# A two-layer hybrid mixer trunk on one core: operations recorded first, then issued in the order of a list scheduler inside the kernel

## Chip, cores and metric

One core of one Trainium2 chip. The metric is the device time of one execution in microseconds, as the median of three runs. All inputs and outputs are float32.

## What is computed

Two layers. Each normalises x (512 tokens, 1024 channels), projects it with one matrix, runs four mixers on their own columns, gates each with a SiLU path, projects the concatenation back and adds it to x. A last normalisation ends it.

```python
def hybrid_layer(x, norm_w, w_in, w_out, conv_w, pe_cmp, w_cmp_k, w_cmp_v, pool_w, pool_scale):
    h = rmsnorm(x, norm_w)
    p = split_cols(h @ w_in)
    o_a = dsa_mixer(...)        # ReLU indexer, 8 heads -> top 128 keys of each query -> softmax attention, 4 heads
    o_b = nsa_mixer(...)        # compressed blocks + selected blocks + window of 512, sigmoid gates, 4 heads
    o_c = shortconv_mixer(...)  # b * conv3(c * x)
    o_d = pool_mixer(...)       # causal means over 2, 4, 8, 16 tokens, minus the token, a linear map per group
    mixed = concatenate([silu(gate) * o for each of the four])
    return x + mixed @ w_out

def reference(x, ...):
    for l in range(2):
        x = hybrid_layer(x, ...)
    return rmsnorm(x, final_norm_w)
```

## The kernel before

The engines are PE (matmuls and transposes), DVE (VectorE), ACT (ScalarE), POOL (GpSimd) and SP, which issues all DMAs. Tokens lie in four tiles of 128. A float32 product of good accuracy is made of three matmuls: every operand is split into a high part (a rounded copy, type float32r) and a low part (the difference, made by `lo`), and high x high, high x low and low x high are added up in PSUM (`lin_tok`, L129, and `lin_ch`, L141).

`load_w` (L98) brings a group of weight columns in four parts: SP loads into a staging tile `st` (four places), ACT copies the high part `wh`, POOL subtracts the low part `wl` (six places each). A staging place is free again when POOL has subtracted.

A layer runs in this program order. `projections` (L678) goes through four groups of columns and, within each, through the four token tiles, four at a time in flight: `group_a` (queries and key of mixer A, index key), `group_idx` (index queries, then per head one score matmul, a relu on ACT into a tile `rl`, two places, and a multiply-add on DVE into `acc`), `group_bk` and `group_bq` (keys, values and queries of mixer B). Then come `compress`, `gates`, and the attention calls `att_a(i)` and `att_b(i)` of token tile i, mixed with `topk` (16 rounds of max and match-replace on DVE over `acc`), `conv` and `conv_gate_pool`. `probs` (L501) makes a call's probabilities in tiles `pb` of the tag `big` (ten places): score matmuls on PE, a reduction on DVE (L519), an exponential on ACT (L521), a reciprocal chain on DVE (L522 to L525), a scaling on POOL (L528). `pv` (L531) transposes them on PE, splits them on ACT and DVE, and multiplies by the values; `finish` (L543) gates the result into `mT`. `att_a(i)` for i > 0 needs `topk(i)`.

At the end of a layer the residual tiles `x` (eight of `big`) and the next norm's gain `g` (two of `rl`) are loaded, and `w_out` is applied in three chunks of columns. In layer 0 the sum goes to `x1d` in DRAM, and each token tile is normalised for layer 1 (`norm_tile`). In layer 1 it is normalised and stored.

The program order is only a wish: the tile framework, which was started with `schedule_with_timeline_sim=True` (L793), orders each engine's instructions by its own model of their durations, and gives a tile one of its tag's places when it comes to it. Nothing moves at run time: each engine runs its list in order, with semaphore waits.

## Time and profile before

| what | value |
|---|---|
| median of three runs | 569.18 us (567.56 to 570.59) |
| the profiled execution, its own time | 571.24 us |
| its span, first to last instruction | 569.5 us |
| mean granted TensorE clock | 0.98 |
| DMA | 51.14 MB, mean 90 GB/s |

The profile counts an engine as busy while one of its instructions runs. Matmuls overlap each other, so a busy PE is not a PE at its peak rate. "Granted clock" is the share of TensorE's full clock that was let through. Behind an instruction group stands the idle time of the engine just before it, and who ended it. The slices of the page (40 equal ones, in tenths) show the shape of the run:

```profile
PE   6989799989999999989999988999999999989995
DVE  3856889999998988963175869999999999795533
PEclk8899989998999999999999989999999999999999
```

### The profile page before, as it was taken

What the parts mean: (1) busy time and instruction counts of PE and PEld (TensorE: products, weight loads), DVE (VectorE), ACT (ScalarE), POOL (GpSimd) and SP (SyncE); (2) the same over time, 40 slices, a digit from 0 to 9 for tenths busy, and PEclk for the clock granted to TensorE, in tenths of its full rate; (3) what the DMA queues carried; (4) which work ended last, traced back from release to release, by engine and by line L of the source; (5) the groups of instructions that cost most, each with busy time, mean ns of one, the idle gap of its engine ahead of it and who ended that gap; (6) DMA issues with size and microseconds to landing.
All of it is one profiled execution on the core that took longest, in us unless ns stands there. A gap on an engine that the chain in (4) does not pass through costs nothing.

```text
span 569.5 us, 9672 instructions
## 1 busy us (share of the span) xinstructions
PE 533.6 (94%) x3076; PEld 469.3 (82%) x3076; DVE 449.4 (79%) x1152; ACT 319.8 (56%) x797; POOL 298.9 (52%) x398
## 2 busy tenths in 40 slices
PE   6989799989999999989999988999999999989995
PEld 5889798768887878779999978886788888878895
DVE  3856889999998988963175869999999999795533
ACT  3466955363645756673345686636544675766243
POOL 4855633473726384551855637427553649454252
PEclk8899989998999999999999989999999999999999
DMA  8632211382313020425722513117513212042303
GB/s 258 201 94 56 64 30 39 83 203 67 75 38 75 20 92 13 138 76 164 196 77 60 135 52 92 39 22 195 137 38 75 55 58 86 28 129 74 111 2 147
DMA packets 70370, 51.14 MB, mean 90 GB/s; under 512 B 19248, under 2 KB 64432, under 8 KB 70320
## 3 DMA queue, kind: packets, MB, share of 16 engines
q1 hardware_dynamic: 70320, 50.54, 32.1%
q8 instruction: 24, 0.39, 0.3%
q14 instruction: 26, 0.21, 0.1%
HBM read 46.33 MB, written 4.19 MB: 89 GB/s over the span
## 4 chain that ended last, share of the span: by engine, by line
PE 60%; DVE 26%; ACT 5%; DMA 3%; issue 2%; POOL 1%; SPq 1%; POOLq 0%; ACTq 0%; DVEq 0%
PE mm L137 9%; PE mm L139 9%; PE mm L138 8%; PE mm L147 7%; PE mm L149 7%; PE mm L148 7%; DVE acc L346 4%; DVE m L345 4%; DVE acc L335 4%; PE tr L535 3%; PE pv L541 2%; PE pv L540 2%; PE s L516 2%; PE s L515 2%; ACT wh L122 2%
## 5 line engine op out<-in xcount | busy, mean ns | idle before, releaser
L95 POOL TENSOR_TENSOR wl<-st,wh 128x768 fp32r<-128x768 f32 (+4 forms) x94 | 161.1, 1734 | 73.6 <-ACT wh L122 63.8
L147 PE MATMUL mm<-hT,wh 128*128 128x512 f32 x272 | 109.4, 402 | 3.0 <-DVE sg L499 1.5
L149 PE MATMUL mm<-hT,wl 128*128 128x512 f32 x272 | 108.3, 400 | 0.8 <-POOL wl L95 0.8
L148 PE MATMUL mm<-hT,wh 128*128 128x512 f32 x272 | 108.4, 399 | 0.0
L528 POOL TENSOR_SCALAR pb<-pb,rs 128x512 f32<-128x512 f32 (+3 forms) x96 | 52.9, 568 | 88.6 <-DVE rs L525 38.3
L521 ACT ACTIVATE pb<-pb,mn 128x512 f32<-128x512 f32 (+3 forms) x96 | 53.7, 559 | 66.7 <-DVE mn L519 63.8
L137 PE MATMUL mm<-wh,hT 128*128 128x360 f32 (+3 forms) x240 | 76.0, 319 | 7.8 <-ACT hT L252 4.2
L122 ACT ACTIVATE wh<-st 128x768 fp32r<-128x768 f32 (+4 forms) x92 | 70.5, 775 | 15.8 <-PE mm L139 7.7
L139 PE MATMUL mm<-wh,hT 128*128 128x360 f32 (+3 forms) x240 | 75.9, 316 | 1.2 <-DVE hT L95 1.2
L138 PE MATMUL mm<-wl,hT 128*128 128x360 f32 (+3 forms) x240 | 75.1, 314 | 0.0
L147 PEld LDWEIGHTS mm<-hT,wh 128*128 128x128 f32 x272 | 51.8, 190 | 14.2 <-DVE sg L499 1.7
L137 PE MATMUL mm<-wh,mT 128*128 128x384 f32 (+1 forms) x192 | 62.0, 324 | 1.0 <-ACT mT L552 0.5
L139 PE MATMUL mm<-wh,mT 128*128 128x384 f32 (+1 forms) x192 | 61.0, 319 | 0.9 <-DVE mT L95 0.9
L138 PE MATMUL mm<-wl,mT 128*128 128x384 f32 (+1 forms) x192 | 61.6, 321 | 0.0
L149 PEld LDWEIGHTS mm<-hT,wl 128*128 128x128 f32 x272 | 51.7, 190 | 11.7 <-POOL wl L95 1.7
L148 PEld LDWEIGHTS mm<-hT,wh 128*128 128x128 f32 x272 | 51.7, 190 | 9.8 <-issue 0.2
L137 PEld LDWEIGHTS mm<-wh,hT 128*128 128x128 f32 x240 | 47.3, 198 | 9.4 <-ACT hT L252 4.7
L345 DVE MAX8 m<-acc 128x8 f32<-128x384 f32 (+2 forms) x96 | 52.2, 551 | 0.4
L346 DVE MATCH_REPLACE8 acc<-m,acc 128x384 f32<-128x384 f32 (+2 forms) x96 | 51.9, 541 | 0.1
L139 PEld LDWEIGHTS mm<-wh,hT 128*128 128x128 f32 x240 | 47.2, 197 | 2.0 <-DVE hT L95 2.0
L95 DVE TENSOR_TENSOR pl<-tr,ph 128x512 fp32r<-128x512 f32 x60 | 40.6, 683 | 10.2 <-ACT ph L538 10.1
L138 PEld LDWEIGHTS mm<-wl,hT 128*128 128x128 f32 x240 | 47.2, 197 | 0.2
(194 smaller groups left out, 1163.9 us busy)
## 6 DMA issues: line engine op xcount, KB each, us to landing
st<-in_w_in_dram SPq DMA_DIRECT2D x104, 128.0 KB, 2.7
st<-in_w_in_dram SPq DMA_DIRECT2D x28, 256.0 KB, 3.3
st<-in_w_out_dram SPq DMA_DIRECT2D x16, 384.0 KB, 3.4
x<-in_x_dram SPq DMA_DIRECT2D x16, 256.0 KB, 4.0
st<-in_w_in_dram SPq DMA_DIRECT2D x8, 320.0 KB, 4.7
st<-in_w_out_dram SPq DMA_DIRECT2D x8, 256.0 KB, 2.9
x1d<-x SPq DMA_DIRECT2D x8, 256.0 KB, 2.0
x<-x1d SPq DMA_DIRECT2D x8, 256.0 KB, 3.2
```

Source lines behind the costliest of these rows:

```text
L95: eng.tensor_sub(dst, src, f(hi))
L122: S.activation(wh[:, :, :n], st[:, :, :n], AF.Copy)
L137: PE.matmul(ps[:, :n], act[0][:, k, ts], rh, start=st, stop=False)
L138: PE.matmul(ps[:, :n], act[0][:, k, ts], rl, start=False, stop=False)
L139: PE.matmul(ps[:, :n], act[1][:, k, ts], rh, start=False, stop=sp)
L147: PE.matmul(ps, lh, act[0][:, k, :], start=k == 0, stop=False)
L148: PE.matmul(ps, lh, act[1][:, k, :], start=False, stop=False)
L149: PE.matmul(ps, ll, act[0][:, k, :], start=False, stop=k == KC - 1)
L345: V.max(m8, a)
L346: V.match_replace(a, m8, a, MARK)
L521: S.activation(p, p, AF.Exp, scale=-1.0, bias=mn[:, h : h + 1], accum_out=rs[:, h : h + 1])
L528: G.tensor_scalar(p, p, rs[:, h : h + 1], 0.0, op0=OP.mult, op1=OP.add)
```

## The change

The kernel now writes a tape. `Tape.record` takes every call to an engine, notes the tiles and the regions that it reads and writes, and makes it wait for the earlier operations that touch the same regions. `Tape.cost` gives each a duration. `Tape.schedule` then picks, again and again, for each engine the recorded operation that can start soonest; among those that can start within 1 ns of that, the one that stands first in program order. `Tape.play` issues the calls in this order, with the framework's own ordering off (`tc.manual_schedule()`).

A tile no longer has a pool's place that the framework hands out, but a slot of its tag, a tag and pool entry of its own, that the scheduler binds when the first operation on it is picked. `Place.safe` lets a tile take a slot ahead of earlier ones only as long as each tile that stands before it in program order can still get one. Weights are recorded where they are first used (`Weights`), and the loads of the compression weights moved from `compress` to `compressed`. In the changed kernel every instruction carries the line of `play`, L422.

```diff
+class Place:
+    def __init__(self, pool, tag, bufs):
+        self.pool, self.tag, self.bufs = pool, tag, bufs
+        self.free = [0.0] * bufs
+        self.holds = [None] * bufs
+        self.waiting = []
+
+    def safe(self, t):
+
+        for k, y in enumerate(self.waiting):
+            if y is t:
+                return True
+            live = sum(1 for h in self.holds if h is not None and h.last >= y.first)
+            live += sum(1 for z in self.waiting[:k] if z.last >= y.first)
+            if live + 2 > self.bufs:
+                return False
...
+class Weights:
+    def __getitem__(self, h):
+        if h not in self.parts:
+            self.parts[h] = self.part(h)
+        return self.parts[h]
...
+SEM = 52
...
+    def cost(self, op):
...
+                if dt == F32R:
+                    op.occ = max(112, m * 0.4375 + 5)
+                    op.seen = m * 0.4375 + 205
...
+        elif op.eng == "ACT":
+            op.dur = (170 if psum else 295 if op.args[2] == AF.Exp else 205) + 0.835 * n
+            op.occ = op.dur - 100
...
+            elif op.name == "tensor_tensor_reduce":
+                op.dur = 208 + 1.04 * n
+                op.occ = op.dur - 84
+            elif op.name in ("tensor_scalar", "tensor_copy") and not psum:
+                op.dur = 146 + 0.52 * n
+                op.occ = op.dur - 84
+                op.locks = True
+            else:
+                op.dur = (215 if op.name == "scalar_tensor_tensor" and not psum else 150) + 1.04 * n
+                op.occ = op.dur - 84
+                op.locks = two
...
+    def schedule(self):
...
+        def candidate(e):
+            best = None
+            soonest = 1e18
+            found = []
+            for op in ready[e]:
+                s = slots(op)
+                if s is None:
+                    continue
+                s = max(s, op.ready, free[e])
+                found.append((s, op))
+                soonest = min(soonest, s)
+            for s, op in found:
+                if s <= soonest + 1 and (best is None or op.num < best[1].num):
+                    best = (s, op)
+            return best
...
+            s, e = min(have)
+            op = cand[e][1]
+            if op.locks:
+                s = max(s, lock["POOL"])
+            if e == "POOL":
+                s = max(s, lock["DVE"])
+            op.start = s
+            if op.locks:
+                lock["DVE"] = s + op.dur
+            if e == "POOL":
+                lock["POOL"] = s + op.dur
+            free[e] = s + op.occ
...
+    def play(self):
+        for op in self.schedule():
+            def real(v):
+                return v.real() if isinstance(v, View) else v
+
+            getattr(self.engines[op.eng].real, op.name)(*[real(a) for a in op.args],
+                                                        **{k: real(v) for k, v in op.kw.items()})
...
-    nc = tc.nc
+    tape = Tape(tc.nc)
...
+    class Pool:
+        def tile(self, shape, dtype, name, tag=None, bufs=None):
+            return tape.tile(self, shape, dtype, name, tag or name, bufs or self.bufs)
...
-        parts = []
...
-        for h in range(4):
+        def part(h):
...
-            parts.append((wh, wl))
-        return parts
+            return wh, wl
+
+        return Weights(part)
...
-        compressed(*cmp_in)
+        compressed(cmp_in)
...
     for l in range(DEPTH):
         st = layer(l, *st)
+    with tc.manual_schedule():
+        tape.play()
```

## The prediction

> **What bounds the kernel now.** First the page's busy table, then the same by stage (windows: length, busy time and instruction count of PE, PEld, DVE, ACT, POOL, then granted clock, DMA share, GB/s).

> ```profile
> PE 533.6 (94%) x3076; PEld 469.3 (82%) x3076; DVE 449.4 (79%) x1152; ACT 319.8 (56%) x797; POOL 298.9 (52%) x398
> ...
> 0.00:30.00 30.00, 23.52 (x124) 21.86 (x125) 18.92 (x32) 13.32 (x36) 19.42 (x44) 0.89 0.76 227
> 30.00:100.00 70.00, 63.47 (x413) 59.18 (x412) 56.19 (x142) 46.61 (x124) 34.06 (x55) 0.98 0.21 54
> 100.00:250.00 150.00, 143.91 (x764) 117.78 (x763) 136.74 (x370) 85.28 (x202) 81.14 (x90) 0.98 0.30 80
> 250.00:330.00 80.00, 79.22 (x527) 77.18 (x525) 41.91 (x93) 39.97 (x108) 44.13 (x57) 1.00 0.45 127
> 330.00:350.00 20.00, 16.64 (x106) 15.59 (x107) 14.83 (x32) 17.22 (x50) 12.91 (x21) 0.91 0.25 66
> 350.00:500.00 150.00, 147.04 (x788) 122.68 (x788) 142.60 (x398) 86.08 (x201) 81.21 (x93) 1.00 0.28 73
> 500.00:550.00 50.00, 46.51 (x259) 41.97 (x258) 31.75 (x74) 25.11 (x64) 20.10 (x30) 1.00 0.27 82
> 550.00:569.50 19.50, 13.29 (x107) 13.09 (x105) 6.50 (x16) 6.26 (x17) 5.91 (x12) 0.94 0.29 108
> ```

> PE is the bound: idle for only 569.5 - 533.6 = 35.9 us of its span. But the second bound is close. In the two attention stages (100 to 250 in layer 0, 350 to 500 in layer 1) DVE is busy 91% and 95%, so PE and DVE are both nearly full there. In 30 to 100, 330 to 350 and 500 to 550 neither is full: there each waits for the other's answers, which is where an order of issue can lose or win. Of the idle time 6.5 us lie in the first 30 us (waiting for the first loads) and 6.2 us in the last 19.5 (the last tiles' scaling and store). The other 23.2 us are 6.5, 6.1, 0.8, 3.4, 3.0 and 3.5 us, row by row.

> Then one such wait from close by: DVE and PE on the timeline around 70 us (start, length, what, and in brackets the idle time before and who ended it), and the windows over the three stretches of low clock after the start.

> ```profile
> 62.39 0.48 DVE L335 SCALAR_TENSOR_TENSOR acc<-rl,wi,acc 128x256 f32<-128x256 f32 x1
> ...
> 65.44 1.87 DVE L335 SCALAR_TENSOR_TENSOR acc<-rl,wi,acc 128x256 f32<-128x256 f32 x1
> ...
> 67.80 1.48 DVE L335 SCALAR_TENSOR_TENSOR acc<-rl,wi,acc 128x256 f32<-128x256 f32 x1
> 69.31 0.42 DVE L95 TENSOR_TENSOR kTB<-tr,kTB 128x256 fp32r<-128x256 f32 x1
> ...
> 69.79 0.44 PE L415 MATMUL tr<-ident,z 128*128 128x128 f32 x2 [1.54 <-DVE kTB L95]
> ...
> 71.75 0.44 PE L415 MATMUL tr<-ident,z 128*128 128x128 f32 x2 [1.08 <-DVE qiT L95]
> ...
> 72.30:75.80 3.50, 3.50 (x16) 3.50 (x15) 3.50 (x12) 1.04 (x3) 1.69 (x5) 0.51 0.33 75
> 126.90:133.80 6.90, 6.54 (x20) 5.24 (x20) 6.90 (x20) 1.78 (x5) 5.86 (x6) 0.51 0.47 109
> 331.70:335.20 3.50, 3.36 (x15) 3.36 (x16) 2.70 (x8) 3.12 (x11) 1.44 (x5) 0.51 0.02 5
> ```

> The same multiply-add of 128x256 takes 0.48 us once and 1.87 and 1.48 us a moment later, so something outside DVE holds it. Behind it in DVE's queue stands the 0.42 us subtraction that frees a transpose bank, and PE, whose next instruction needs that bank, idles 1.54 us and soon 1.08 us more. Right after it the granted clock is 0.51 for 3.5 us. The three stretches are 13.9 us at half rate, so they cost 13.9 x 0.49 = 6.8 us: 1.7, 3.4 and 1.7. An order that avoids the short waits also saves these.

> [...]

> **The change part by part.** It adds and drops no arithmetic: the same matmuls, DVE, ACT and POOL operations, the same DMAs. Both programs are statically ordered per engine; what changes is the order, and which tile gets which buffer when.

> (1) The order by fitted durations. Place one, PE in layer 0, at the wait of 69.8 us: block key transposes (`tr<-ident,z`), index scores (`s<-kiT,qiT`), projections (`mm`). Before:

> ```order
> L332 MATMUL s_777<-kiT_180,qiT_709 128x384
> L415 MATMUL tr_956<-ident,z_918 128x128 x2
> L332 MATMUL s_782<-kiT_180,qiT_709 128x384
> L332 MATMUL s_787<-kiT_180,qiT_710 128x384
> L415 MATMUL tr_1050<-ident,z_961 128x128 x2
> L137 MATMUL mm_1108<-wh_1025,hT_139 128x320
> ```

> Now:

> ```order
> L422 MATMUL mm_954<-wh_679,hT_192 128x268
> L422 MATMUL tr_992<-ident,z_879 128x128 x2
> L422 MATMUL mm_954<-wh_679,hT_181 128x268
> L422 MATMUL s_1002<-kiT_426,qiT_780 128x384
> L422 MATMUL mm_954<-wl_698,hT_181 128x268
> L422 MATMUL mm_954<-wh_679,hT_192 128x268
> ```

> Before, two pairs of transposes that need DVE's answers stood almost back to back; now 20 projection matmuls and one score stand between this pair and the next. Such waits are what this part can remove. Outside the attention stages the idle time is 6.5 + 0.8 + 3.4 + 3.5 = 14.2 us, and two of the low-clock stretches lie there, 1.7 + 1.7 = 3.4 us: 17.6 us together. I take three quarters, 13 us (10.6 of waits, 2.6 of clock): the waits are of order, but new ones will come. Bounds: nothing, and 17.6 us. In the attention stages there are 6.1 + 3.0 us of idle PE and 3.4 us of clock, 12.5 us. DVE is 91 and 95% full there and does the same work after as before, so I take 2 us, with the bounds nothing and 12.5. What holds DVE (the 1.87 us) stays: the new scheduler reckons with it, but does not choose around it, since it adds that delay after it has chosen.

> (2) Buffers taken early. Place two, SP's queue in layer 0, after the query weights; `x` are the residual tiles that the output projection adds at the end of the layer (before they were issued 43 rows later, behind the output weights), `g` the next norm's gain. Before:

> ```order
> L111 DMA st_1043<-in_w_in_dram 128x2x64
> L447 DMA pet_1300<-in_pe_cmp_dram 16x2x64
> L111 DMA st_1247<-in_w_in_dram 128x2x128
> L111 DMA st_1247<-in_w_in_dram 128x2x256
> L111 DMA st_1254<-in_w_in_dram 128x2x128
> ```

> Now:

> ```order
> L422 DMA pet_455<-in_pe_cmp_dram 16x2x64
> L422 DMA x_463<-in_x_dram 128x512
> L422 DMA x_469<-in_x_dram 128x512
> L422 DMA x_480<-in_x_dram 128x512
> L422 DMA x_493<-in_x_dram 128x512
> L422 DMA x_509<-in_x_dram 128x512
> L422 DMA x_523<-in_x_dram 128x512
> L422 DMA g_535<-in_norm_w_dram 128x512
> L422 DMA pet_782<-in_pe_cmp_dram 16x2x64
> L422 DMA st_877<-in_w_in_dram 128x2x128
> ```

> Six residual tiles and a gain now stand ahead of the compression weights (`st_877`). The transfers are cheap: six of 256 KB while the DMA engines are 21% busy. They hold buffers, though: 6 of the 10 `big` places and 1 of the 2 `rl` places until the layer's end, and in layer 1 the reads of `x1d` do the same. So the four 512-wide probability tiles of one attention call fill all that is left, and relu (ACT) and multiply-add (DVE) of the index scores share one buffer. Prices, from the groups by form (count, busy us, mean ns of one):

> ```profile
> L519 DVE CUSTOM_DVE_ANT_0 pb<-s,acc 128x512 f32<-128x512 f32 x8 | 5.5, 689 | 2.8 <-PE s L516 2.7
> L521 ACT ACTIVATE pb<-pb,mn 128x512 f32<-128x512 f32 x24 | 17.3, 722 | 21.1 <-DVE mn L519 21.1
> L521 ACT ACTIVATION_READ_ACCUMULATOR pb<-pb,mn 128x1 f32 x96 | 18.1, 189 | 0.0
> L522 DVE TENSOR_SCALAR rs<-rs 128x4 f32<-128x4 f32 x24 | 12.6, 523 | 1.6 <-ACT pb L521 1.5
> L523 DVE RECIPROCAL rs<-rs 128x4 f32<-128x4 f32 x24 | 4.1, 170 | 0.2
> L528 POOL TENSOR_SCALAR pb<-pb,rs 128x512 f32<-128x512 f32 x24 | 16.3, 696 | 31.2 <-DVE mx L590 11.6 <-DVE rs L523 10.0 <-DVE rs L525 8.8
> L95 DVE TENSOR_TENSOR pl<-tr,ph 128x512 fp32r<-128x512 f32 x60 | 40.6, 683 | 10.2 <-ACT ph L538 10.1
> L546 ACT ACTIVATE ob<-pv 64x512 f32<-64x512 f32 x16 | 9.5, 595 | 10.5 <-PE pv L541 8.3 <-PE pv L602 1.8
> L334 ACT ACTIVATE rl<-s 128x256 f32<-128x256 f32 x16 | 6.2, 389 | 0.2
> L334 ACT ACTIVATE rl<-s 128x384 f32<-128x384 f32 x16 | 7.9, 492 | 7.4 <-PE s L332 6.0 <-DVE acc L335 1.4
> L334 ACT ACTIVATE rl<-s 128x512 f32<-128x512 f32 x16 | 9.5, 594 | 2.4 <-PE s L332 2.2
> L335 DVE SCALAR_TENSOR_TENSOR acc<-rl,wi,acc 128x256 f32<-128x256 f32 x14 | 11.7, 836 | 0.5 <-ACT rl L334 0.3
> L335 DVE SCALAR_TENSOR_TENSOR acc<-rl,wi,acc 128x384 f32<-128x384 f32 x14 | 10.3, 734 | 1.1 <-ACT rl L334 1.1
> L335 DVE SCALAR_TENSOR_TENSOR acc<-rl,wi,acc 128x512 f32<-128x512 f32 x14 | 11.5, 821 | 0.0
> ```

> With one `rl` buffer the relu no longer runs under the multiply-add: per layer 8 x (0.389 + 0.492 + 0.594) = 11.8 us more in a chain of 8 x (0.836 + 0.734 + 0.821) = 19.1 us. I cost it at nothing: DVE is 56.19 of 70 us busy there, its own other work fills the gaps, and PE has projections left. With that cover gone, it is 11.8 us a layer, and top-k of tile 1 is late next.

> Place three, DVE in layer 0, between the third and the fourth tile's attention on selected keys (`att_a(2)`, `att_a(3)`; `ISA pb,mn<-s,acc` is the reduction of the scores). Before:

> ```order
> L551 SCALAR_TENSOR_TENSOR om_2149<-om_2149,sg_1480 128x256
> L522 TENSOR_SCALAR rs_2463<-rs_2463 128x4
> L523 RECIPROCAL rs_2463<-rs_2463 128x4
> L95 TENSOR_TENSOR mT_1246<-om_2149,mT_1245 128x2x128
> L519 ISA pb_2917,mn_2921<-s_2923,acc_847 128x512
> L519 ISA mn_2921 128x1
> ```

> Now:

> ```order
> L422 TENSOR_TENSOR pl_2963<-tr_2926,ph_2937 128x512
> L422 TENSOR_TENSOR cd_2897<-cd_2917,tab 128x16
> L422 TENSOR_TENSOR om_2983<-pv_2912,ob_2974 64x256 x2
> L422 TENSOR_TENSOR cd_2897<-cd_2897,cd_2880 128x16
> L422 SCALAR_TENSOR_TENSOR om_2983<-om_2983,sg_1399 128x256
> L422 SCALAR_TENSOR_TENSOR cd_2917<-cd_2917,mm_2878 128x512
> L422 ISA pb_2995,mn_2996<-s_2960,acc_1246 128x512
> ```

> Before, tile 3's reductions followed tile 2's reciprocal almost at once; now they come after tile 2's transposes, products and gate. Tile 3's chain, now alone: 4 x 0.69 + 0.72 + 0.19 + 0.52 + 0.17 + 0.70 + 4 x 0.68 + 0.60 = 8.4 us per layer. I cost it at nothing, since PE still has the last convolution gate and half of the output projection's matmuls then, and tile 2's scores stand 47 rows earlier in PE's queue than before. If that cover fails it is 8.4 us a layer, 16.8 in all; the last token tile's output projection is late next.

> At the layer boundary two reads of `x1d` now stand in SP's queue ahead of the last of layer 1's first weights, and each must wait until the store before it has landed:

> ```profile
> x1d<-x SPq DMA_DIRECT2D x8, 256.0 KB, 2.0
> ```

> That is 2 x 2.0 = 4 us for the queue. I cost it at nothing, because PE is busy 79.22 of 80 us there with output projection; were that cover gone, it is 4 us, once, and layer 1's first projection is late next.

> Recording, constants set earlier on POOL and the weights asked for at first use cost nothing: POOL is idle 10.6 of the first 30 us.

> **The sum.** 13 + 2 = 15 us off. The profiled execution took 571.24 us with a span of 569.5, 2.1 us above the median 569.18; taken from the median, the forecast is **554 us**, own range 539 (all 30.1 us of movable idle and clock) to 569 (none).

> **The rivals.**

> First, DVE sets the time: the attention stages stay as they are, and what is won elsewhere only lets DVE's queue start waiting earlier. For it: 91 and 95%. Against it: outside of attention DVE is 56.19 of 70, 14.83 of 20 and 31.75 of 50. Time: only the 2 us, 567.

> Second, held buffers. One place, the end of each layer's attention: tile 3 starts its reductions only when tile 2's four places are free, PE runs out of matmuls that do not need tiles 2 and 3, and DVE has no top-k left. For it: the rows of place three, and 500 to 550, where PE already loses 3.5 us at this place. Against it: PE's cover. It decides from the point where the chain, 8.4 us, outlasts PE's other work. With it the relu chain of one buffer is exposed to a third, 2 x 11.8 / 3 = 7.9. Time: 569.2 + 16.8 + 7.9 - 13 = 581.

> Third, the fit is better than I grant, and all 30.1 us go. For it: the durations in the new cost table are near the rows here (208 + 1.04 x 512 ns = 0.74 us for the 512-wide reduction, beside 0.69 above). Against it: two engines that are both over 90% full seldom leave no gap. Time: 539.

> Fourth, the change doesn't do what it says: a greedy order that fails on the chip where DVE is held from outside: new waits replace old ones one for one. Time: 569.

> **How the numbers follow.** Forecast 0.52, better fit 0.13, DVE or one for one 0.11, held buffers 0.24. Within 0.5% (566.3 to 572.0, about what this measurement can tell from no change) fall DVE's case and the one-for-one case, 0.11 together; faster is 0.52 + 0.13 = 0.65; slower 0.24. The range is 539 to 579: it leaves out the lower half of the better fit and about half of the held buffers.

> **What would show it.** Right: PE idle in 30 to 100 and about 330 to 350 shrinks by some 10 us, at most one half-rate stretch after the start, DVE's attention stages as long as before. Wrong: ACT's relu waiting for DVE's multiply-add in the waits view, DVE's reductions waiting for PE's transposes, or an idle PE just ahead of the last token tile's output projection. A PE span that shrinks by over 25 us would say that attention was not bound by DVE.

## The result, and the profile after

The changed kernel takes 596.11 us (594.85 to 598.99) where the kernel before takes 569.88 in the same session: a ratio of 1.0467, interval 1.0407 to 1.0526. It is 26 us slower, and outside the predicted range. The profiled execution took 594.85 us with a span of 593.1.

The page of the changed kernel: busy time by engine, and the slices of PE, DVE and the granted clock.

```profile
PE 547.8 (92%) x3076; PEld 470.2 (79%) x3076; DVE 428.1 (72%) x1152; ACT 320.8 (54%) x797; POOL 302.5 (51%) x398
...
PE   7997999999999789999999789999999899898995
...
DVE  4764689989899898452374658899998978475423
...
PEclk9996999999999899999999979999999979898999
```

DVE is busy 21.3 us less than before (449.4), for the same operations (e1 below, the new machinery with the old order, has 448.9): the new order avoids some of the holds (83 DVE instructions take over 1.25 times the median of their form before, 65 now; they stand 68.5 and 49.0 us above it in all). Nothing came of it. PE idles 593.1 - 547.8 = 45.3 us instead of 35.9, and what it does it does at a lower clock (mean 0.969, before 0.980). By stage (window, length, busy time and count of PE, PEld, DVE, ACT, POOL, clock, DMA share, GB/s):

```profile
30.00:100.00 70.00, 63.70 (x391) 57.16 (x389) 50.51 (x124) 45.42 (x122) 37.95 (x56) 0.93 0.30 81
100.00:250.00 150.00, 140.03 (x709) 109.30 (x709) 130.72 (x370) 80.70 (x189) 75.92 (x84) 0.99 0.26 67
250.00:330.00 80.00, 77.53 (x504) 74.49 (x504) 39.38 (x91) 39.15 (x105) 42.48 (x58) 1.00 0.44 129
330.00:350.00 20.00, 15.41 (x93) 13.69 (x91) 10.01 (x30) 14.28 (x39) 5.17 (x7) 0.83 0.30 73
350.00:500.00 150.00, 144.56 (x797) 120.49 (x798) 134.70 (x406) 87.08 (x215) 78.06 (x93) 0.98 0.29 70
500.00:550.00 50.00, 45.16 (x210) 36.41 (x209) 29.86 (x61) 25.24 (x51) 29.09 (x33) 0.93 0.22 69
```

A window of fixed times mixes different work in the two kernels. Both issue the same PE instructions, so progress can be compared directly. Weight each one by its duration in the new cost table (504 us in all), and note when so much of it had been issued, in us from the start (e1 to e13 are the experiments below):

```
PE work issued     25     50    100    150    175    275    300    400    450    500
before           39.5   71.8  129.6  181.7  207.9  314.8  346.7  452.6  504.9  559.3
after            36.4   73.6  126.9  179.2  218.0  325.6  361.9  465.7  528.4  582.9
after - before   -3.1   +1.8   -2.7   -2.5  +10.1  +10.8  +15.2  +13.1  +23.5  +23.6
e1               39.8   72.0  128.7  180.1  206.3  313.2  344.4  450.4  502.7  557.3
e2               37.6   79.1  134.7  185.7  212.3  319.1  360.0  464.6  519.9  575.3
e4               37.8   75.9  129.2  180.6  211.6  324.3  359.8  463.5  516.8  571.9
e5               38.1   67.2  120.2  170.6  204.8  310.1  340.0  444.3  506.9  557.9
e6               38.0   67.2  120.7  170.9  197.8  303.4  333.4  444.8  498.0  550.9
e7               40.0   72.2  125.8  176.0  205.0  313.3  344.5  452.6  512.5  567.1
e13              37.4   71.5  124.3  175.2  207.0  317.8  351.0  455.5  522.1  578.3
```

The loss lies at four places: two index stages (about 40 to 70 us, +4.9; 326 to 362, +4.4) and two late attention stages (179 to 218, +12.6; 466 to 528, +10.4). Elsewhere the changed kernel is even or a little ahead.

The first place, close by: ACT, DVE and PE on the timeline of the changed kernel, in the split of the index queries `qiT` (start, length, what; in brackets the idle time before and who ended it).

```profile
45.32 0.76 ACT L422 ACTIVATE qiT<-tr 32x256 fp32r<-32x256 f32 x2
46.22 0.42 DVE L422 TENSOR_TENSOR qiT<-tr,qiT 32x256 fp32r<-32x256 f32 x1
46.66 0.76 ACT L422 ACTIVATE qiT<-tr 32x256 fp32r<-32x256 f32 x2 [0.59 <-DVE qiT L422]
...
46.69 0.39 PE L422 MATMUL s<-kiT,qiT 96*128 96x256 f32 x1 [1.81 <-DVE qiT L422]
47.46 0.42 DVE L422 TENSOR_TENSOR qiT<-tr,qiT 32x256 fp32r<-32x256 f32 x1 [0.83 <-ACT qiT L422]
47.91 0.76 ACT L422 ACTIVATE qiT<-tr 32x256 fp32r<-32x256 f32 x2 [0.49 <-DVE qiT L422]
48.71 0.42 DVE L422 TENSOR_TENSOR qiT<-tr,qiT 32x256 fp32r<-32x256 f32 x1 [0.83 <-ACT qiT L422]
49.16 0.77 ACT L422 ACTIVATE qiT<-tr 32x256 fp32r<-32x256 f32 x2 [0.49 <-DVE qiT L422]
```

From 46.66 us on, ACT and DVE take strict turns: each starts 30 to 40 ns after the other ends, 1.25 us a step. In the scheduler's plan the four DVE instructions start at 42.34, 42.81, 43.37 and 43.94 us, 0.5 us a step, with ACT working beside them. ACT's second pair reads another part of the transpose bank `tr` and writes another part of `qiT` than DVE does, so the recorder saw no reason to wait. The built program has one: a semaphore wait of ACT on DVE at that instruction.

Taking all semaphore waits of the changed program and removing those that the recorder's own dependencies, its places and each engine's order already force, 100 waits between engines are left that the scheduler did not know of. 38 are these between ACT and DVE on the index queries. All have one form: an engine waits because another one used the same PSUM bank before it, even if both only read it, or use different parts.

The program guards by bank: ACT's second pair above reads partitions 32 to 63 of `tr`, DVE partitions 0 to 31, and ACT starts 20 ns after DVE's end, after 0.59 us of idling. Whether the two could overlap is not shown: no run here tried it.

The second place: the view of DVE's `m` (the maxima of top-k), between 100 and 260 us, before and then after. The first and last start stand behind "first and last start us" in its heading, here the two times with "to".

```profile
L345 DVE MAX8 m<-acc x32: 404/611/697, 99.6 to 166.0; 128x8 f32<-128x512 f32 x16, 128x8 f32<-128x384 f32 x12, 128x8 f32<-128x256 f32 x4
```

```profile
L422 DVE MAX8 m<-acc x37: 408/556/695, 101.3 to 208.3; 128x8 f32<-128x512 f32 x16, 128x8 f32<-128x384 f32 x13, 128x8 f32<-128x256 f32 x8
```

The 16 rounds of 512 are token tile 3's. The last of them starts at 166 us before and at 208 now (439 and 484 in layer 1). With its replacements a top-k of this width is some 22 us of DVE work (16 rounds of two instructions of some 0.68 us) that nobody needs before `att_a(3)`; now it sits among the attention calls of tiles 1 and 2. The windows over the same PE work in layer 0 (150 to 175 us of it), before and then after:

```profile
181.70:207.90 26.20, 25.38 (x125) 21.19 (x124) 23.35 (x64) 16.08 (x40) 16.88 (x20) 1.00 0.14 41
```

```profile
179.20:218.00 38.80, 32.07 (x145) 22.18 (x145) 35.66 (x115) 19.67 (x53) 13.56 (x22) 0.96 0.05 14
```

DVE is nearly full in both, and in the second it does 12.3 us more for the same PE work: about the 12.6 us that the stage lost. PE's longest wait there is for a scaling on POOL, which itself had waited 5.69 us for DVE:

```profile
193.43 0.40 PE L422 MATMUL pv<-ph,vc 96*128 96x512 f32 x1
195.97 2.17 POOL L422 TENSOR_SCALAR pb<-pb,rs 128x384 f32<-128x384 f32 x3 [5.69 <-DVE mx L422]
196.81 0.44 PE L422 MATMUL tr<-ident,pb 128*128 128x128 f32 x2 [2.98 <-POOL pb L422]
```

Layer 1's late attention looks different. DVE does 47.47 us of work in its 62.7 us, where before it did 46.15 in 52.3, so it is not full. PE's first long wait there (2.59 us) is for a scaling that stood in POOL's queue behind the subtraction of weights:

```profile
467.38 4.38 POOL L422 TENSOR_TENSOR wl<-st,wh 128x768 fp32r<-128x768 f32 x2 [1.03 <-ACT wh L422]
471.75 2.55 POOL L422 TENSOR_SCALAR pb<-pb,rs 128x384 f32<-128x384 f32 x4
472.67 2.24 PE L422 MATMUL tr<-ident,pb 128*128 128x128 f32 x8 [2.59 <-POOL pb L422]
```

The experiments tie this loss, too, to the order of the attention; by which wait it comes about is not shown.

### The profile page after: what moved, and what is told of

It reads as the page before. It is cut to its first block, busy times and chain, and to the rows that moved or that the text cites. A ratio compares the mean times of both kernels' runs of the same rounds, so it can differ in the third digit from the quotient of the medians.

```text
span 593.1 us, 9664 instructions
## 1 busy us (share of the span) xinstructions
PE 547.8 (92%) x3076; PEld 470.2 (79%) x3076; DVE 428.1 (72%) x1152; ACT 320.8 (54%) x797; POOL 302.5 (51%) x398
## 4 chain that ended last, share of the span: by engine, by line
PE 71%; DVE 14%; ACT 7%; issue 4%; POOL 3%; DMA 1%; SPq 1%; POOLq 0%; ACTq 0%; DVEq 0%
PE mm L422 52%; PE tr L422 7%; PE s L422 5%; PE pv L422 4%; ACT qiT L422 2%; PE ms L422 2%; POOL pb L422 2%; DVE pb L422 2%; DVE acc L422 2%; DVE cd L422 1%; DVE om L422 1%; DVE rs L422 1%; DVE qiT L422 1%; DVE pl L422 1%; DMA x<-in_x_dram 1%
## 5 line engine op out<-in xcount | busy, mean ns | idle before, releaser
L422 POOL TENSOR_TENSOR wl<-st,wh 128x768 fp32r<-128x768 f32 (+4 forms) x94 | 161.5, 1734 | 60.4 <-ACT wh L422 29.3
L422 PE MATMUL mm<-hT,wh 128*128 128x512 f32 x544 | 180.0, 401 | 0.0
L422 PE MATMUL mm<-wh,hT 128*128 128x360 f32 (+3 forms) x480 | 112.8, 316 | 3.5 <-ACT qiT L422 1.5
L422 PEld LDWEIGHTS mm<-hT,wh 128*128 128x128 f32 x544 | 101.6, 190 | 18.1 <-DVE cd L422 0.2
L422 PE MATMUL mm<-hT,wl 128*128 128x512 f32 x272 | 108.7, 401 | 0.0
L422 POOL TENSOR_SCALAR pb<-pb,rs 128x512 f32<-128x512 f32 (+3 forms) x96 | 55.2, 592 | 94.2 <-DVE rs L422 69.2
L422 PE MATMUL mm<-wh,mT 128*128 128x384 f32 (+1 forms) x384 | 93.1, 324 | 0.5 <-ACT mT L422 0.5
L422 PEld LDWEIGHTS mm<-wh,hT 128*128 128x128 f32 x480 | 83.7, 197 | 5.2 <-ACT z L422 1.9
L422 ACT ACTIVATE wh<-st 128x768 fp32r<-128x768 f32 (+4 forms) x92 | 71.0, 778 | 25.0 <-PE mm L422 17.3
L422 PE MATMUL mm<-wl,hT 128*128 128x360 f32 (+3 forms) x240 | 75.1, 315 | 1.4 <-POOL wl L422 1.3
L422 PEld LDWEIGHTS mm<-wh,mT 128*128 128x128 f32 x384 | 67.4, 191 | 2.2 <-DVE cd L422 0.8
L422 ACT ACTIVATE ph<-tr 128x512 fp32r<-128x512 f32 (+1 forms) x68 | 38.0, 594 | 52.7 <-PE tr L422 52.4
L422 PE MATMUL mm<-wl,mT 128*128 128x384 f32 (+1 forms) x192 | 61.3, 321 | 0.0
L422 ACT ACTIVATE pb<-pb,mn 128x512 f32<-128x512 f32 (+3 forms) x96 | 53.2, 557 | 14.9 <-DVE mn L422 14.6
L422 PE MATMUL tr<-ident,pb 128*128 128x128 f32 x240 | 47.8, 290 | 12.3 <-POOL pb L422 11.2
L422 PEld LDWEIGHTS mm<-hT,wl 128*128 128x128 f32 x272 | 51.5, 189 | 8.9
L422 PEld LDWEIGHTS tr<-ident,pb 128*128 128x128 f32 x240 | 30.9, 146 | 28.4 <-POOL pb L422 22.2
L422 DVE TENSOR_TENSOR pl<-tr,ph 128x512 fp32r<-128x512 f32 x60 | 39.3, 684 | 18.9 <-ACT ph L422 18.7
L422 DVE MATCH_REPLACE8 acc<-m,acc 128x384 f32<-128x384 f32 (+2 forms) x96 | 51.7, 541 | 0.0
L422 DVE MAX8 m<-acc 128x8 f32<-128x384 f32 (+2 forms) x96 | 51.0, 549 | 0.2
L422 PEld LDWEIGHTS mm<-wl,hT 128*128 128x128 f32 x240 | 47.3, 197 | 2.3 <-POOL wl L422 1.8
L422 DVE TENSOR_TENSOR x<-mm,x 128x256 f32<-128x256 f32 (+2 forms) x32 | 12.8, 421 | 40.0 <-PE mm L422 39.9
## 6 DMA issues: line engine op xcount, KB each, us to landing
st<-in_w_in_dram SPq DMA_DIRECT2D x28, 256.0 KB, 3.1
x<-in_x_dram SPq DMA_DIRECT2D x16, 256.0 KB, 4.5
st<-in_w_out_dram SPq DMA_DIRECT2D x8, 256.0 KB, 2.7
x1d<-x SPq DMA_DIRECT2D x8, 256.0 KB, 3.1
x<-x1d SPq DMA_DIRECT2D x8, 256.0 KB, 3.2
```

The source lines that it names most:

```text
L422: getattr(self.engines[op.eng].real, op.name)(*[real(a) for a in op.args], **{k: real(v) for k, v in op.kw.items()})
```

## The experiments

Theory A: the new order of attention, above all the late top-k. Theory B: places taken early (the prediction's part 2 and its second rival). Theory C: the machinery, whatever the order. Theory D: the bank waits that the scheduler does not know. Theory E: the half-rate clock after short waits.

| run | us (median) | ratio to the kernel before, interval |
|---|---|---|
| e1_old_order | 568.76 | 0.9973 (0.9946 to 1.0000) |
| e2_gain_late | 587.91 | 1.0306 (1.0260 to 1.0352) |
| e3_residual_and_gain_late | 603.59 | 1.0561 (1.0524 to 1.0597) |
| e4_topk_recorded_first | 582.96 | 1.0193 (1.0154 to 1.0233) |
| e5_bank_rule | 568.13 | 0.9977 (0.9951 to 1.0003) |
| e6_bank_rule_topk_early | 562.85 | 0.9879 (0.9821 to 0.9936) |
| e7_old_order_topk_late | 579.27 | 1.0170 (1.0119 to 1.0220) |
| e8_before_held | 618.15 | 1.0849 (1.0771 to 1.0927) |
| e9_waits_filled | 587.44 | 1.0303 (1.0255 to 1.0351) |
| e10_bank_rule_topk_early_late_places | 588.41 | 1.0305 (1.0245 to 1.0365) |
| e11_search_1 | 563.37 | 0.9879 (0.9842 to 0.9915) |
| e12_search_2 | 559.50 | 0.9805 (0.9759 to 0.9850) |
| e13_rule_for_index_queries | 590.89 | 1.0380 (1.0333 to 1.0426) |

### e1: the old order in the new machinery

Every recorded operation was matched to its instruction in the program before, and `schedule` returns that order; places are still fixed slots. (The lines with dots stand for longer code.)

```diff
-        order = []
-        ...greedy choice...
+        for n, k in enumerate(ORDER):    # the order of the kernel before
+            op = ops[k]
...
+        return [ops[k] for k in ORDER]
```

> The recorded operations are issued in the order in which the kernel before issued them, engine by engine; tiles keep fixed places. Theory A (the new order is at fault, above all the top-k of token tile 3, which DVE finishes at 209 us instead of 167 in layer 0 and at 484 instead of 440 in layer 1): 570 us, within 4. Theory B (places taken early): also 570, since this order takes the residual tiles and the gain late. Theory C (the new machinery itself costs: fixed places, more semaphore waits): 590 to 596.

Measured 568.76 us, no slower than before. Theory C falls: fixed places and an order issued by hand cost nothing. All 26 us are in the order, with the places that are taken early in it. The old order has nearly as many of those waits (90 between engines by the same count), but they cost less: DVE idles 7.8 us in all for ACT ahead of its subtractions on `qiT` before, and 15.0 in the changed kernel.

### e2 and e3: gain and residual tiles taken late

```diff
     def safe(self, t):
+        if t.name.startswith(("g_",)):     # e3: ("x_", "g_")
+            return self.waiting[0] is t
```

> Only the gain tiles g may no longer pass other tiles of their tag, so both places of rl serve the index scores. Theory B (places taken early): the index stages lose 9 us (layer 0) and 9 us (layer 1) against the scheduler's own plan; with the second place most of that is won back, 580 to 586 us. Theory A (order of the top-k): the attention losses of 12 and 10 us stay, and the index stages lose the same through transposes and half-rate clock: 591 to 597.

Measured 587.91, 2 us from where theory B put it, but not for its reason. The single `rl` buffer did make ACT wait, and with the second place that wait is gone. The waits view, the changed kernel and then e2:

```profile
ACT rl L422 <- DVE acc L422: 11.9, 11, 1.9
```

```profile
ACT rl L423 <- DVE acc L423: 1.3, 2, 1.0
```

Yet the index stages won nothing. PE is busy less in them than in the changed kernel (59.89 for 63.70 of 70 us), and the gain is in the attention, here layer 0's (147.62 for 140.03 of 150):

```profile
30.00:100.00 70.00, 59.89 (x367) 55.04 (x366) 50.23 (x120) 44.08 (x119) 35.25 (x54) 0.90 0.29 76
100.00:250.00 150.00, 147.62 (x797) 120.95 (x796) 131.76 (x386) 84.56 (x200) 81.53 (x89) 1.00 0.28 73
```

The edit shifted the greedy order, and tile 3's top-k happens to end at 161 and 450 us in it (the end of its last replacement), not at 211 and 485. That is theory A's effect. The number alone, which lies between the two ranges and nearer to B's, would have pointed to the wrong theory.

> Gain and residual tiles take their places only when all tiles of their tag that stand ahead in program order have theirs. Theory B (places taken early): 575, both effects gone. Theory A: no gain beyond that of the gain tiles alone, 585 to 600; the scheduler's own sum of durations ends later with this edit (576 against 567).

Measured 603.59: against B. With the residual tiles late as well it is 15.7 us slower than e2, and top-k of tile 3 ends at 198 and 490 us.

### e4: top-k recorded first

```diff
+        topk(1)
+        topk(2)
+        topk(3)
         att_b(3)
         att_a(0)
-        topk(1)
         att_a(1)
         att_b(1)
         att_b(2)
-        topk(2)
-        topk(3)
         att_b(0)
```

> The three top-k calls are recorded ahead of the first attention call; scheduler, costs and places unchanged, six residual tiles and a gain are still taken early. Theory A: DVE finishes the top-k of tile 3 some 40 us sooner, PE no longer starves at 180 to 215 us, 15 to 22 us less: 574 to 581. Theory B: the holds are all still there, so at most 5 us change: 591 to 597.

Measured 582.96, 13 us less than the changed kernel; A said 574 to 581, so it is right in sign and 2 us outside. Tile 3's top-k ends at 160 and 439 us. By the progress table the late attention of layer 0 loses 4.8 us against before (between 150 and 175 us of work) instead of 12.6, and layer 1's (400 to 450) 1.0 instead of 10.4. The index stages still lose, and 6 us are lost anew at layer 0's end (175 to 275).

### e5: the scheduler is told of the bank waits

```diff
                     if (w or writes) and a < r1 and r0 < b and had & bits:
                         op.before[o.num] = o
+                    if v.tile.place.pool.name == "pp" and o.eng != op.eng:
+                        op.before[o.num] = o
```

> The recording layer now also makes an operation wait for every earlier operation of another engine on the same PSUM bank, reads and other regions of it too, as the built program's semaphores already do: in the changed kernel 100-odd waits stand that the scheduler did not know of, 38 of them between ACT and DVE on the index queries' bank. Theory D (these unplanned waits stretch the index stages): the drift between plan and chip in 40 to 60 and 320 to 360 us falls from 17 us to 8 or less, and the whole to 576 to 583; DVE still ends tile 3's top-k late (plan: 179 us), so part of theory A's loss stays. Theory A alone: index stages as long as before this edit, 590 to 596.

Measured 568.13, 28 us less than the changed kernel, more than D said. No wait between engines is left in the program that the scheduler does not know. To see where, compare plan and chip: start on the chip less planned start, on PE, in us.

```
at about (us)      40     60    320    360    end    index stages together
after             1.6    9.2   13.6   22.7   26.5    16.7
e2                2.8   10.2   14.5   23.4   23.9    16.3
e4                2.9   10.6   19.8   28.1   30.4    16.0
e5                2.8    4.7    7.6    9.9   10.6     4.2
e13               2.5    5.9   12.2   17.1   24.0     8.3
```

The index stages ran 16.7 us longer than planned in the changed kernel, and 4.2 here. The same stages by windows of e5:

```profile
30.00:100.00 70.00, 67.46 (x432) 61.28 (x431) 56.53 (x149) 49.62 (x131) 37.73 (x56) 1.00 0.29 78
...
330.00:350.00 20.00, 19.78 (x137) 18.75 (x136) 16.84 (x37) 13.72 (x39) 12.33 (x20) 1.00 0.27 66
```

PE gains 3.8 of 70 and 4.4 of 20 us over the changed kernel, and the clock is full in both. On the timeline of e5 the split of the index queries is no longer bunched; ACT and DVE have other work between the turns:

```profile
46.83 0.42 DVE L424 TENSOR_TENSOR qiT<-tr,qiT 32x256 fp32r<-32x256 f32 x1 [0.23 <-ACT qiT L424]
47.91 0.43 DVE L424 TENSOR_TENSOR qa<-tr,qa 64x256 fp32r<-64x256 f32 x1 [0.66 <-ACT qa L424]
48.70 0.42 DVE L424 TENSOR_TENSOR qiT<-tr,qiT 32x256 fp32r<-32x256 f32 x1 [0.36 <-ACT qiT L424]
```

The relu still waits for the multiply-add in e5, so the single `rl` buffer is not what stretched these stages:

```profile
ACT rl L424 <- DVE acc L424: 8.5, 12, 2.0
```

Of the span's 25.0 us less, 9.0 are in the plan (566.5 to 557.5) and 15.9 in the drift (26.5 to 10.6). Tile 3's top-k still ends late (186 and 469 us), and e5 gives back 8 and 10 us against before in the two late attention stages.

### e6 and e7: the late top-k by itself

e6 is e5 with another order of recording.

```diff
+        topk(1)
         att_b(3)
+        topk(2)
         att_a(0)
-        topk(1)
+        topk(3)
         att_a(1)
         att_b(1)
         att_b(2)
-        topk(2)
-        topk(3)
         att_b(0)
```

> The bank rule of the run before, and the three top-k calls recorded between topk(1), att_b(3), topk(2), att_a(0), topk(3), ahead of the other attention calls. Theories A and D together: both losses shrink, 565 to 573, that is the kernel before or a little less. A without D: 577 to 583. D without A: no better than the run before.

Measured 562.85, 5.3 us less than e5 and 2 us below what was expected, and 1.2% under the kernel before. The progress table shows it at the late attention, which takes 26.9 us instead of 34.2 in layer 0 (150 to 175 us of work) and 53.2 instead of 62.6 in layer 1 (400 to 450). In layer 1, of the 13.3 us that it is ahead of the kernel before at 300 us of work, 5.5 are lost again by 400.

e7 takes the old order of e1 and moves only the instructions of tile 3's top-k.

```diff
-ORDER = ...old order...
+ORDER = ...old order, with the 33 DVE instructions of topk(3) in each layer
+           spread over the times at which the changed kernel ran them...
```

> The old order in fixed places (568.8 us), with one thing moved: the top-k of token tile 3 is spread on DVE over the times at which the changed kernel ran it (it ends near 207 us instead of 168, and near 476 instead of 442). No operation is added. Theory A (late top-k takes DVE time from what PE needs next): 8 to 20 us longer, 577 to 589. Against A: within 3 us, 566 to 572, since no other operation needs this top-k before att_a(3).

Measured 579.27, 10.5 us more than e1, and the view of `m` shows the one thing that moved:

```profile
L473 DVE MAX8 m<-acc x32: 402/617/695, 99.8 to 206.7; 128x8 f32<-128x512 f32 x16, 128x8 f32<-128x384 f32 x12, 128x8 f32<-128x256 f32 x4
```

This is theory A alone, with no buffer, wait or cost touched: the same DVE work at another time costs 10.5 us. The progress table says where. In layer 0 PE first runs 4.1 us ahead of e1, on the DVE time that the top-k left (at 150 us of work), and is level again at 275. Layer 1 pays it all: 2.2 us behind at 400, 9.8 at 450. So in layer 0 a late top-k alone only moves time about; how much of the changed kernel's loss there is the top-k, and how much what its index stage had left undone, these runs don't separate.

### e8 and e10: places taken early, in two other orders

e8 is the kernel before, under its own ordering, with three pairs of residual tiles and one gain tile loaded ahead of the index queries.

```diff
             for i in range(NT):
                 yield norm_a(i, w_first)
+            xn.extend(x_tile() for _ in range(3))
+            for i in range(3):
+                load_x(xn[i], xsrc, i)
+            g.append(load_g1(0))
...
```

> The kernel before, its own ordering, with the loads of three pairs of residual tiles and of one gain tile recorded ahead of the index queries, so that 6 of 10 places of big and 1 of 2 of rl are held until the layer's end, as in the changed kernel. Theory B (places taken early cost time by themselves): 580 to 592. Against B (other work fills in, the loss is of the order): 567 to 575.

Measured 618.15: far more than B said. PE is short of work at the layer ends, the place the prediction's second rival had named:

```profile
250.00:330.00 80.00, 70.50 (x407) 65.29 (x406) 35.55 (x82) 35.20 (x93) 36.97 (x53) 0.96 0.37 108
...
500.00:550.00 50.00, 44.20 (x216) 34.80 (x214) 36.25 (x114) 28.02 (x74) 22.14 (x30) 0.93 0.08 27
```

In the first row PE is busy 70.50 us where the kernel before has 79.22.

e10 is e6 with the edit of e3.

> The kernel with the bank rule and the early top-k (562.9 us), in which residual tiles and gain may no longer take places ahead of other tiles of their tag. Theory B (places taken early cost time): 550 to 560. Against B (the scheduler works around the holds; loads that wait until all probability tiles have places only come late): 572 to 585; the scheduler's own sum is 572.5 instead of 553.

Measured 588.41, 25.6 us more than e6. Of these, 19.5 are in the scheduler's own sum (553.0 to 572.5). So with the early loads the old program is some 48 us slower, and without them the new one is 26 us slower. Both edits shift everything else too, so neither number is the price of a buffer.

### e9: the waits filled

The list of every engine as in the changed kernel; ahead of 24 PE instructions that waited there, 0.5 to 3 us each, stand transposes of the identity. They are 241, not 224 as the expectation says.

```diff
+    for n in FILL:
+        idle = bank("ms", 1)
+        for _ in range(n):
+            PE.transpose(idle[:, :P], ident, ident)
```

> The order of the changed kernel, every engine's list unchanged, with 224 transposes of the identity that nobody reads put on PE ahead of 24 instructions that waited 0.6 us or more there, as many as fit into each measured wait. Theory E (the short waits halve the clock, 34 us at half rate in the changed kernel against 14 before, and that is 8 to 10 us of its loss): half-rate stretches after the start fall to 10 us or less, 583 to 589. Against E (in those stretches PE waits for others anyway, so half rate costs nothing): 594 to 600.

Measured 587.44, 8.7 us less than the changed kernel, with 241 more instructions. From the page:

```profile
PE 562.8 (96%) x3317; PEld 487.1 (83%) x3317; DVE 428.4 (73%) x1152; ACT 320.8 (55%) x797; POOL 303.7 (52%) x398
...
PEclk8899999999999999999999999999999999999999
```

Between the head and the last 3 us the clock is never halved. In the changed kernel six stretches after the head were at half rate (10.2, 3.4, 6.8, 6.8, 3.4 and 3.4 us, 34.1 in all), so a half-rate microsecond cost 0.26 us there, where the prediction had taken 0.49. In 4.9 us of these stretches PE was idle; what made up the rest of the difference was not tried. By the progress of PE, without the added transposes, layer 0's late attention still takes 38.0 us (38.8 in the changed kernel, 26.2 before) and layer 1's 59.2 (62.7 and 52.3). So the clock is a small part of that loss in layer 0, and a third of it in layer 1.

### e11 and e12: can the plan be trusted now

Both are e5 with another order of recording, e11 also with a tie window of 20 ns, found by trying such orders on the cost model. e12's:

```diff
+        topk(1)
+        topk(2)
+        att_b(1)
         att_b(3)
         att_a(0)
-        topk(1)
+        topk(3)
         att_a(1)
-        att_b(1)
         att_b(2)
-        topk(2)
-        topk(3)
         att_b(0)
```

> The bank rule, attention calls recorded in the order topk 2, topk 1, att_b 3, att_a 0, topk 3, att_b 2, att_a 1, att_b 1, att_b 0, and a tie window of 20 ns instead of 1. The scheduler's own sum is 544.0; the two kernels with the bank rule ran 9.9 and 10.6 us above theirs. If the sum can now be trusted (theories A and D are all of it): 552 to 557. If gains of the plan are again lost to waits that it does not know: 560 to 568.

> The bank rule, attention calls recorded in the order topk 1, topk 2, att_b 1, att_b 3, att_a 0, topk 3, att_a 1, att_b 2, att_b 0, tie window 1 ns. The scheduler's own sum is 546.2. As in the run before: 554 to 559 if the sum can be trusted, 560 to 568 if not.

e11 measured 563.37, e12 559.50. e12 is the best kernel here, 10.2 us faster than the one before; e11, planned 9 us shorter than e6, is not faster than e6. The four kernels with the bank rule stand 19.4, 13.3, 9.9 and 10.6 us above their plans (e11, e12, e6, e5). e11 falls on the side of "not", e12 half a microsecond outside the range of "trusted". A gain of a few us in the plan is no promise. e12's page:

```profile
PE 530.7 (95%) x3076; PEld 462.7 (83%) x3076; DVE 424.0 (76%) x1152; ACT 320.8 (57%) x797; POOL 301.2 (54%) x398
```

PE idles 27.8 us in it, 8.1 less than before.

### e13: the rule for the index queries alone

```diff
                         op.before[o.num] = o
+                    if o.eng != op.eng and all(z.outs[0].tile.name.startswith("qiT") for z in (o, op)):
+                        op.before[o.num] = o
```

> The scheduler learns only of the waits between ACT and DVE in the split of the index queries (38 of the 100-odd that it did not know); all others stay unknown. Its own sum is 564.6 us against 566.5 without it, so on paper nothing is gained, and it still ends tile 3's top-k late (179 us in the plan). Theory D, placed in the index stages: the drift of 17 us there falls to 8 or less, 580 to 586. Against it (the gain of the full rule, 28 us, came from elsewhere, or only from another order of the attention): 590 to 597.

Measured 590.89: as a total it falls on the side against D. By stage it does not. The index stages run 8.3 us over their plan instead of 16.7, and at 300 us of work e13 is 10.9 us ahead of the changed kernel (351.0 for 361.9). Then it loses 14 us against before in layer 1's late attention (2.9 at 400 us of work, 17.2 at 450), with top-k of tile 3 ending at 478 us and half-rate clock:

```profile
350.00:500.00 150.00, 144.01 (x756) 117.28 (x755) 138.15 (x392) 83.29 (x199) 74.26 (x85) 0.95 0.27 67
```

So telling of these 38 waits takes away half of the index stages' excess. The rest of e5's 28 us comes with the other 62 waits and with the order that the greedy choice then makes; these two were not tried apart.

## Why the prediction was wrong

**The bound** was read rightly: PE is it, DVE is close behind in attention. The sentence drawn from it failed: "DVE is 91 and 95% full there and does the same work after as before, so I take 2 us, with the bounds nothing and 12.5". A nearly full engine was taken as a floor on both sides. The work in all stayed the same, but a part of it moved: in layer 0's late attention DVE had 12.3 us more to do, the stage lost 12.6 us, and an order of recording that ends the top-k early takes the loss away (e6 beside e5). Layer 1's stage lost 10.4 us; there, too, the runs in which the top-k ends early (e2, e4, e6) are free of most of it. The bounds had no loss in them at all.

**Step (1), 13 us of waits and clock** outside attention, is the term that failed worst. It took three quarters of all idle time for granted: "the waits are of order, but new ones will come". The idle time in 30 to 100 and 330 to 350 went from 6.5 and 3.4 us to 6.3 and 4.6, and half-rate clock after the head from 13.9 to 34.1 us. What was missing is a question on the new scheduler: which waits does its recorder know? It knows regions; the program waits by bank. If the cost model goes through the lists of the changed kernel as they are, with the 100 unknown waits added, it ends at 582.0 us instead of 566.5. Of these 15.5 us, 10.5 fall between 40 and 60 and between 320 and 360 us, where the chip ran 16.7 us over the plan. The fitted durations were near enough: over the whole trace ACT's sum is within 5%. The waits were not. What the step said of the clock, that it hangs on the short waits, held: with the waits filled, it is not halved between head and end (e9: 1.00 in every stage from 30 to 550 us).

**The plan** was never priced against the old order. The same cost model, going through the old order's lists in the same way, gives 571.6 us for it, and 566.5 for the new one. So it puts the new order 5.1 us ahead, where on the chip its span is 25.6 us longer (593.1 beside e1's 567.5): 31 us the wrong way. With the unknown waits of each added it gives 574.2 and 582.0, and so ranks them rightly. The plan also had the loss of the late attention in it: from 150 to 175 us of work the new order takes 39.9 us in the model and the old one 29.1, from 400 to 450 it is 63.2 and 58.8.

**Step (2), early places at nothing**, comes out near the truth in the changed kernel, though not by the cover that it named. The relu waits for the multiply-add appeared as foretold (11.9 us), and taking them away won nothing in the index stages (e2). The two reads of `x1d` cost 1 us of PE progress at most (9.8 to 10.8 us behind before, between 250 and 275 us of work). The chain of tile 3's attention is behind tile 2's, as the rows of place three said; in layer 0 it runs after the top-k, and from 175 to 275 us of work the loss is 0.7 us. But in layer 1 the held places do bite once. A reduction of DVE waits for PE's transposes, which free one of the four places of `big` that the residual tiles do not hold, and PE then waits for what comes of it:

```profile
510.23 0.56 DVE L422 CUSTOM_DVE_ANT_0 pb<-s,acc 128x384 f32<-128x384 f32 x1 [5.90 <-PE tr L422]
516.04 1.25 PE L422 MATMUL tr<-ident,pb 128*128 128x128 f32 x4 [2.88 <-POOL pb L422]
```

**The second rival, held buffers,** had the right sign and came nearest with 581, by a mechanism that is at most a small part of it (the 2.88 us above, and the half-rate stretch at 515.5 us behind them): forbidding all the holds made the kernel slower, twice (e3, e10). Its price is real in the old ordering, and larger than it said (e8). **The fourth, one for one,** had the right mechanism, new waits in place of old, but no size: it did not count the clock or the late top-k.

The 25.6 us can be put together from parts measured apart. The plans differ by 5.1 us in favour of the new order. The bank waits add 12.9 (15.5 for the new order, 2.6 for the old). The other 17.8 are in no plan: half-rate clock, 8.7 by the medians of e9, and 6.7 by which the model, with the waits, prices the old order above its span. This last excess lies in the late attention (58.8 us for 52.3 between 400 and 450 us of work); its cause wasn't tried. 2.4 us stay open. The late top-k, worth 10.5 us in the old order (e7), is no further part: it stands in the plan already. The parts are not independent. Telling the scheduler of the waits alone undoes all of the loss (e5), and 9.0 of the 25.0 us by which e5's span is shorter lie in the other plan that it then makes.

**What was to show it right or wrong**: the signs named for "wrong" were well chosen. Two of them appeared, relu behind multiply-add and DVE's reductions behind PE's transposes, but neither is the main cause.

## What to carry to other kernels

Before a hand-made order is trusted, compare the waits in the built program with those that the planner knows; one missing rule on shared PSUM banks added 15.5 us to the model's time here, as much as the forecast hoped to win. Price the old order with the new planner's costs, stage by stage: if the model ranks the two otherwise than the chip, or loses in a stage what it won before, its gains are not gains. A list scheduler that breaks ties by program order must be told, by that order, which long work on a nearly full engine is needed last; and one edit in it shifts everything, so judge an experiment by the stage that it was aimed at, not by the total.

## What the runs showed of the hardware

```profile
44.50:47.90 3.40, 1.59 (x14) 1.39 (x13) 1.68 (x4) 2.25 (x6) 0.00 (x0) 1.00 0.00 0
47.90:58.10 10.20, 7.66 (x31) 6.48 (x30) 5.72 (x15) 8.28 (x21) 2.08 (x2) 0.50 0.00 1
194.60:198.10 3.50, 0.88 (x4) 0.41 (x4) 3.05 (x12) 0.42 (x1) 2.13 (x3) 0.99 0.00 0
198.10:201.50 3.40, 3.30 (x10) 2.34 (x11) 3.06 (x9) 1.28 (x3) 0.60 (x2) 0.50 0.00 0
471.10:474.50 3.40, 1.46 (x7) 0.75 (x8) 3.40 (x9) 0.00 (x0) 3.40 (x6) 1.00 0.83 214
474.50:481.30 6.80, 6.27 (x18) 4.51 (x18) 4.22 (x11) 3.56 (x9) 2.01 (x1) 0.50 0.23 63
```

PE was busy 1.59, 0.88 and 1.46 us, and half rate followed at once. The longest waits in or into these three windows were 1.81, 2.98 and 2.59 us, each shorter than the grid's 3.413 us.
